# Hybrid decoder trunk on Trainium2: the first adaLN vectors summed by TensorE in place of VectorE and GpSimd

## The chip, the core and the metric

The kernel runs on one core of one Trainium2 chip. The metric is the device time of one execution in microseconds (us); less is better. Engines are named as in the profile: PE is TensorE (its matmuls), PEld TensorE's weight loads, DVE VectorE, ACT ScalarE, POOL GpSimd, and SP the engine whose queue issues most of the DMAs.

## What is computed

Two decoder layers on `x` (256 tokens by 1024 channels, f32). What matters here is how the first layer begins. The vector `c` (1024) goes through SiLU, and a 1024 x 6144 matrix makes six vectors of 1024 of it. The first two, shift and scale, are applied to the RMS-normalised `x`; the result `h` is the input of the first projection.

```
c_act = jax.nn.silu(c)
for layer in range(DEPTH):
    ada = c_act @ w_ada[layer] + b_ada[layer]
    sh1, sc1, g1, sh2, sc2, g2 = jnp.split(ada[:, None, :], N_ADA, axis=-1)
    h = rms_norm(x, norm_mix[layer]) * (1.0 + sc1) + sh1
    x = x + g1 * hybrid_mixer(h, w_in[layer], ...)
    h = rms_norm(x, norm_ffn[layer]) * (1.0 + sc2) + sh2
    x = x + g2 * f
```

`hybrid_mixer` projects `h` with `w_in` (1024 x 9232), runs forgetting attention and an HGRN2 recurrence on parts of the result, and projects back. `f` is a dense SwiGLU in layer 0 and a top-2-of-8 expert SwiGLU in layer 1.

## The kernel before, in words

Weights come from HBM as f32. Each is split into two parts of type fp32r: `halves` (L93) has ACT round the raw tile to `whi`, and `lower` (L97) has DVE subtract that from the raw tile to give `wlo`. A product is then three matmuls, high by high, high by low and low by high (`mm3`, L113 to L115, 512 columns wide, or `turned`, L411 to L413, 256 columns wide). The activations are split in the same way into `hTh` and `hTl`.

The first stage, `start` (L507 to L637), runs before the two things that every product needs are there: `h` needs shift and scale, and these need 8 MB of `w_ada`. So `start` works in four chunks of two blocks of 128 channels (`CHUNKS = (2, 2, 2, 2)`). For chunk q it loads two pieces of `w_ada` (1 MB each, scale then shift; channels of `c` on the partitions, eight rows k for each partition) and three pieces of `w_in` of 0.5 MB for three groups of output columns (`FIRST`). Loads go through SP's queue in program order, two chunks ahead; the raw tiles lie in a ring of eight, and a tile is loaded again when its last reader is done.

For each chunk the vectors are made in three steps before the change:

- `sums(q)`: DVE multiplies the eight rows of the scale piece by `silu(c)` and adds them up (L537, L539, 128 x 256 each), into `ac`.
- `shift_sums(q)`: POOL does the same for the shift piece, by one multiplication in place (L544, 128 x 2048) and three halving additions (L548).
- `columns(q)`: PE sums over the partitions, with the 128 x 128 blocks of `ac` as weights and a column of ones as the moving operand (L556): four f32 matmuls of one column, each of them two records in the trace.

`vectors(q)` then has DVE add the bias and multiply by the gain (L563, L565). ACT and DVE apply the vectors to the transposed, normalised `x` (L612, L614), ACT rounds (L615), DVE makes the low part (L617), and the products of the chunk follow: `products(q, 0)` with 12 matmuls of 512 columns, `products(q, 1)` with 24 of 256 columns, `products(q, 2)` with 12 of 512 columns. `turn(q + 1)` (L577, four transposes of `x`) and `columns(q + 1)` stand between the last two, so that the vectors of the next chunk come while `products(q, 2)` runs. `rows` (L570), `load_params` (L219 to L221) and `build_masks` (L159 to L192, on POOL) are helpers of the stage. `start` is written under a manual schedule: each engine gets its instructions in the order in which the code stands, and each engine works in order.

After the four chunks the mixer goes on with the next projection (`proj`), whose raw tiles come from four of the same ring's places. The layers behind it, in the order of the program, are the mixer, the dense part, the second mixer and the experts.

Of the kernel before, what the change touches and what calls it, by code (L numbers as in the profile page):

```python
# [14 lines left out]
OP = mybir.AluOpType  # L15
AX = mybir.AxisListType

P = 128
D = 1024
KD = D // P  # L20
# [20 lines left out]
def hybrid_trunk_kernel(  # L41
# [7 lines left out]
    v, a, pe, g = nc.vector, nc.scalar, nc.tensor, nc.gpsimd  # L49
# [7 lines left out]
    def acc_bank(name="acc"):  # L57
        return ps.tile([P, 512], F32, tag="acc", bufs=4, name=name)

    def t_bank(name="tb"):  # L60
        return ps.tile([P, 512], F32, tag="tb", bufs=4, name=name)
# [17 lines left out]
    def load_raw(src, nk, n, step=None):  # L79
        raw = raw_tile()  # L80
        if nk * n == 2048:
            raw = raw.rearrange("p (k n) -> p k n", k=nk)
        else:
            raw = raw.rearrange("p (k n) -> p k n", k=max(4, nk))[:, :nk, :n]
        for k in range(0, nk, step or nk):
            nc.sync.dma_start(out=raw[:, k:k + (step or nk)], in_=src[:, k:k + (step or nk)])
        return raw

    def halves(raw, room=None):

        hi, lo = room or (wp.tile([P, 2, 512], F32R, tag=t, bufs=NSP, name=t) for t in ("whi", "wlo"))
        hi, lo = hi[:, :raw.shape[1], :raw.shape[2]], lo[:, :raw.shape[1], :raw.shape[2]]
        a.copy(hi, raw)  # L93
        return raw, hi, lo

    def lower(raw, hi, lo):
        v.tensor_sub(lo, raw, hi.bitcast(F32))  # L97

    def pairs_of(w):
        return [(w[1][:, j], w[2][:, j]) for j in range(w[1].shape[1])]  # L100
# [47 lines left out]
    ones = const.tile([P, P], F32, name="ones")  # L148
# [48 lines left out]
    cact = const.tile([P, KD], F32, name="cact")  # L197
# [98 lines left out]
    def tmp(pool, name):  # L296
        return pool.tile([P, 512], F32, tag="tmp", bufs=4, name=name)
# [207 lines left out]
    def start(pool, hT, win):  # L505

        ring[0] = [wraw, (pool, "kq", 2), (pool, "ee", 2)]  # L507
        wa = w_ada[0].rearrange("(p k) n -> p k n", k=KD)
        wi = win.rearrange("(k p) n -> p k n", p=P)
        first = {c0: [acc_bank() for _ in range(NT)] for c0 in FIRST[:2]}  # L510
        first[FIRST[2]] = [t_bank() for _ in range(NT)]
        NQ = len(CHUNKS)
        first_of = [sum(CHUNKS[:q]) for q in range(NQ)]
        ld, acs, tps, mvs = {}, {}, {}, {}

        def load(q):
            kk, nb = first_of[q], CHUNKS[q]
            raws = []
            for comp in (1, 0):
                raws.append(load_raw(wa[:, :, D * comp + P * kk:D * comp + P * (kk + nb)], KD, P * nb))  # L520
                if q == 0 and comp == 1:
                    nc.sync.dma_start(out=xt, in_=x[0].rearrange("(i p) d -> p i d", p=P))
            ab = raw_tile()
            third = pool.tile([P, 1024], F32, tag=("lfh", "lfl")[q % 2], bufs=2, name="third")
            for c0, t in zip(FIRST, (ab[:, :1024], ab[:, 1024:], third)):
                t = t.rearrange("p (k n) -> p k n", k=2)[:, :nb]
                nc.sync.dma_start(out=t, in_=wi[:, kk:kk + nb, c0:c0 + 512])
                raws.append(t)
            ld[q] = raws

        def sums(q):

            raw, ac = ld[q][0], tmp(pool, "ac")[:, :P * CHUNKS[q]]
            acs[q] = [ac]
            for k in range(KD):
                if k == 0:
                    v.tensor_scalar(out=ac, in0=raw[:, 0], scalar1=cact[:, 0:1], scalar2=None, op0=OP.mult)  # L537
                else:
                    v.scalar_tensor_tensor(out=ac, in0=raw[:, k], scalar=cact[:, k:k + 1], in1=ac, op0=OP.mult, op1=OP.add)  # L539

        def shift_sums(q):

            w = ld[q][1]
            g.tensor_tensor(out=w, in0=w, in1=cact[:, :, None].to_broadcast([P, KD, P * CHUNKS[q]]), op=OP.mult)  # L544
            n = KD
            while n > 1:
                n //= 2
                g.tensor_add(w[:, :n], w[:, :n], w[:, n:2 * n])  # L548
            acs[q].append(w[:, 0])

        def columns(q):
            nb = CHUNKS[q]
            tp = mvs[q] = t_bank()
            for n in range(2):
                for b in range(nb):
                    pe.matmul(out=tp[:, nb * n + b:nb * n + b + 1], lhsT=acs[q][n][:, b * P:(b + 1) * P], rhs=ones[:, 0:1], start=True, stop=True)  # L556

        def vectors(q):
            kk, nb = first_of[q], CHUNKS[q]
            tp = mvs[q]  # L560
            for n, comp in enumerate((1, 0)):
                dst = ada[:, 0, comp, kk:kk + nb]
                v.tensor_add(dst, tp[:, nb * n:nb * (n + 1)], bcol[:, KD * comp + kk:KD * comp + kk + nb])  # L563
                if comp == 1:
                    v.scalar_tensor_tensor(out=dst, in0=dst, scalar=1.0, in1=gain_mix[0][:, kk:kk + nb], op0=OP.add, op1=OP.mult)  # L565

        def rows(k0, k1):
            for i in range(NT):
                cs = slice(P * k0, P * k1)
                a.activation(out=hT.xn[i][:, cs], in_=xt[:, i, cs], func=AF.Copy, scale=hT.r[i])  # L570

        def turn(q):
            tp = tps[q] = t_bank()
            for b in range(CHUNKS[q]):
                for i in range(NT):
                    kk = first_of[q] + b
                    pe.transpose(out=tp[:, (2 * b + i) * P:(2 * b + i + 1) * P], in_=hT.xn[i][:, kk * P:(kk + 1) * P], identity=ident)  # L577

        def products(q, n, w):
            bk = first[FIRST[n]]  # L580
            for c in range(4 if FIRST[n] == O_HQ else NT):
                for b in range(CHUNKS[q]):
                    k = first_of[q] + b
                    if FIRST[n] == O_HQ:
                        turned(bk, c, k, w[b], hT)
                    else:
                        mm3(bk[c], *hT.get(k, c), *w[b], k == 0, k == KD - 1)

        load(0)
        load(1)  # L590
        sums(0)
        for i in range(NT):
            for h in range(2):
                hT.square(i, h)
        for i in range(NT):
            hT.scale(i)
        rows(0, CHUNKS[0])
        shift_sums(0)
        load_params()
        turn(0)  # L600
        columns(0)
        rows(CHUNKS[0], KD)
        for q, nb in enumerate(CHUNKS):
            kk = first_of[q]
            w = [halves(ld[q][2])]
            if q:
                lower(*w[0])
            vectors(q)
            w.append(halves(ld[q][3]))
            hf = tmp(pool, "hf").rearrange("p (b t) -> p b t", b=2)[:, :nb]  # L610
            A, B = (ada[:, 0, j, kk:kk + nb] for j in (1, 0))
            a.activation(out=hf[:, 0], in_=tps[q][:, 0:S], func=AF.Identity, scale=A[:, 0:1], bias=B[:, 0:1])  # L612
            if nb > 1:
                v.tensor_scalar(out=hf[:, 1], in0=tps[q][:, S:2 * S], scalar1=A[:, 1:2], scalar2=B[:, 1:2], op0=OP.mult, op1=OP.add)  # L614
            a.copy(hT.hh[:, kk:kk + nb], hf)  # L615
            lower(*w[q > 0])
            v.tensor_sub(hT.hl[:, kk:kk + nb], hf, hT.hh[:, kk:kk + nb].bitcast(F32))  # L617
            if not q:
                lower(*w[1])
            products(q, 0, pairs_of(w[0]))  # L620
            w.append(halves(ld[q][4]))
            lower(*w[2])
            if q + 2 < NQ:
                load(q + 2)
            if q + 1 < NQ:
                sums(q + 1)
                shift_sums(q + 1)
            products(q, 1, pairs_of(w[1]))
            if q + 1 < NQ:
                turn(q + 1)  # L630
                columns(q + 1)
            products(q, 2, pairs_of(w[2]))
            if q == 0:
                load_late()
            if q == NQ - 2:
                build_masks(pool)
        ring[0] = [wraw]  # L637
        return first

# [1119 lines left out]
    ws = mixer(1, hT, {O_HI: banks[0]}, {O_HI + 512: banks[1]})  # L1759
# [8 lines left out]
CHUNKS = (2, 2, 2, 2)  # L1768
# [37 lines left out]
```

## Time and profile before

| what | value |
|---|---|
| device time, median of 3 runs | 1914.8 us (1912.79 to 1915.34) |
| the profiled execution's own time | 1916.2 us |
| its span in the trace | 1914.5 us |
| PE busy | 1845.4 us (96%) |
| DVE busy | 1569.5 us (82%) |
| ACT busy | 1309.9 us (68%) |
| POOL busy | 210.2 us (11%) |
| mean granted PE clock | 0.993 |
| read from HBM | 522.72 MB, 274 GB/s over the span |

The span runs from the first to the last instruction in the trace; 1.7 us of the profiled execution's own time lie around it. Busy time is a union over an engine's instructions. PEclk, the granted clock, is 1.00 at 2.4 GHz and 0.50 at 1.2 GHz; it is known from the first recorded change on, which in this trace is at 38.1 us, and shown as 1.00 ahead of that.

### The profile page before, as it was taken

Reading aid. Unit: us, or ns where it says so; the run is one execution under the profiler, and the core shown is the slowest. Engines: PE = TensorE matmul, PEld = TensorE weight load, DVE = VectorE, ACT = ScalarE, POOL = GpSimd, SP = SyncE. Lnnn points to the kernel's source line nnn. Section 1 sums busy time; section 2 is a strip of 40 time slices with the busy share of each in tenths; the row PEclk is TensorE's granted clock in tenths of the full one; section 3 lists DMA queues with packets and bytes.
Section 4 is the critical chain, followed back from the end, with each engine's and each line's share of the span. In section 5 each row is a group of like instructions: output and inputs, shape, how many; then the busy total and the mean of one; then the engine's idle time right before and its main releaser. Section 6 shows DMA issues by size and latency. Waiting matters only on the chain.

```text
span 1914.5 us, 25527 instructions
## 1 busy us (share of the span) xinstructions
PE 1845.4 (96%) x9510; PEld 1534.2 (80%) x9510; DVE 1569.5 (82%) x2006; ACT 1309.9 (68%) x1666; POOL 210.2 (11%) x184
## 2 busy tenths in 40 slices
PE   2999999999999999999999999999999999999998
PEld 2787788889978877788787888888888888888887
DVE  6878865878858887457898989999899989999997
ACT  2467568554436765595788787787887878878775
POOL 6701200000000012100001210003100021000000
PEclk9899999999999999999999999999999999999999
DMA  9543654888855425339899999999999999999990
GB/s 301 167 156 132 220 176 142 299 302 293 314 211 172 140 88 176 120 114 338 293 347 354 349 339 370 362 376 344 340 374 359 375 346 344 368 362 369 358 364 24
DMA packets 235140, 525.50 MB, mean 274 GB/s; under 512 B 11756, under 2 KB 23292, under 8 KB 235008
## 3 DMA queue, kind: packets, MB, share of 16 engines
q1 hardware_dynamic: 233624, 523.61, 76.3%
q8 instruction: 76, 1.25, 0.3%
q14 instruction: 56, 0.46, 0.1%
q10 hardware_dynamic: 1384, 0.18, 0.1%
HBM read 522.72 MB, written 1.05 MB: 274 GB/s over the span
## 4 chain that ended last, share of the span: by engine, by line
PE 74%; DVE 2%; ACT 2%; issue 1%; POOL 1%; DVEq 0%; ACTq 0%; POOLq 0%
PE acc L114 15%; PE acc L115 15%; PE acc L113 15%; PE yb L114 5%; PE yb L115 5%; PE yb L113 5%; PE acc L412 2%; PE acc L413 2%; PE acc L411 2%; PE tb L308 2%; DVE wlo L97 1%; PE tb L1560 1%; PE tb L798 1%; POOL rs L302 1%; PE tb L1290 1%
## 5 line engine op out<-in xcount | busy, mean ns | idle before, releaser
L97 DVE TENSOR_TENSOR wlo<-raw,whi 128x1024 fp32r<-128x1024 f32 (+1 forms) x888 | 1077.1, 1237 | 141.7 <-ACT whi L93 124.5
L93 ACT CAST whi<-raw 128x1024 fp32r<-128x1024 f32 (+1 forms) x888 | 919.3, 1047 | 315.3 <-PE acc L115 183.9
L113 PE MATMUL acc<-whi,g 128*128 128x512 f32 x880 | 349.2, 397 | 0.0
L115 PE MATMUL acc<-whi,g 128*128 128x512 f32 x880 | 344.2, 391 | 0.0
L114 PE MATMUL acc<-wlo,g 128*128 128x512 f32 x880 | 344.1, 391 | 0.0
L113 PE MATMUL acc<-whi,hTh 128*128 128x512 f32 x512 | 210.2, 414 | 4.1 <-ACT hTh L615 4.1
L114 PE MATMUL acc<-wlo,hTh 128*128 128x512 f32 x512 | 206.9, 405 | 5.2 <-DVE wlo L97 5.0
L115 PE MATMUL acc<-whi,hTl 128*128 128x512 f32 x512 | 206.6, 405 | 3.5 <-DVE hTl L617 3.5
L114 PEld LDWEIGHTS acc<-wlo,g 128*128 128x128 f32 x880 | 165.5, 188 | 35.9 <-DVE wlo L97 2.8
L115 PEld LDWEIGHTS acc<-whi,g 128*128 128x128 f32 x880 | 165.1, 188 | 35.7
L113 PEld LDWEIGHTS acc<-whi,g 128*128 128x128 f32 x880 | 165.4, 188 | 32.7
L114 PE MATMUL yb<-wlo,th 128*128 128x512 f32 x440 | 172.5, 392 | 4.1 <-DVE wlo L97 4.1
L115 PE MATMUL yb<-whi,tlo 128*128 128x512 f32 x440 | 171.6, 390 | 0.0
L113 PE MATMUL yb<-whi,th 128*128 128x512 f32 x440 | 171.6, 390 | 0.0
L114 PEld LDWEIGHTS acc<-wlo,hTh 128*128 128x128 f32 x512 | 98.2, 192 | 25.4 <-DVE wlo L97 7.5
L115 PEld LDWEIGHTS acc<-whi,hTl 128*128 128x128 f32 x512 | 97.6, 191 | 24.4 <-DVE hTl L617 5.3
L411 PE MATMUL acc<-hTh,whi 128*128 128x256 f32 x416 | 117.1, 282 | 0.0
L302 POOL TENSOR_TENSOR rs<-rs,mhalf 128x8 f32<-128x8 f32 (+1 forms) x28 | 48.1, 1719 | 623.9 <-DVE rs L301 614.9
L413 PE MATMUL acc<-hTh,wlo 128*128 128x256 f32 x416 | 116.5, 281 | 0.0
L412 PE MATMUL acc<-hTl,whi 128*128 128x256 f32 x416 | 116.3, 280 | 0.0
L113 PEld LDWEIGHTS acc<-whi,hTh 128*128 128x128 f32 x512 | 97.4, 191 | 22.4 <-ACT hTh L615 5.0
L114 PEld LDWEIGHTS yb<-wlo,th 128*128 128x128 f32 x440 | 82.6, 188 | 26.0 <-DVE wlo L97 9.3
(381 smaller groups left out, 2634.8 us busy)
## 6 DMA issues: line engine op xcount, KB each, us to landing
raw<-in_moe_w_gate SPq DMA_DIRECT2D x112, 1024.0 KB, 6.3
raw<-in_moe_w_up SPq DMA_DIRECT2D x112, 1024.0 KB, 5.9
raw<-in_moe_w_down SPq DMA_DIRECT2D x110, 1024.0 KB, 5.6
raw<-in_w_in SPq DMA_DIRECT2D x66, 1024.0 KB, 5.2
raw<-in_w_ada SPq DMA_DIRECT2D x48, 1024.0 KB, 6.8
raw<-in_dense_w_gate SPq DMA_DIRECT2D x10, 1024.0 KB, 8.1
raw<-in_dense_w_up SPq DMA_DIRECT2D x10, 1024.0 KB, 7.8
raw<-in_dense_w_down SPq DMA_DIRECT2D x10, 1024.0 KB, 8.8
```

What stands on the lines that cost most here:

```text
L93: a.copy(hi, raw)
L97: v.tensor_sub(lo, raw, hi.bitcast(F32))
L113: pe.matmul(out=o, lhsT=lh, rhs=rh, start=start, stop=False)
L114: pe.matmul(out=o, lhsT=lh, rhs=rl, start=False, stop=False)
L115: pe.matmul(out=o, lhsT=ll, rhs=rh, start=False, stop=stop)
L302: g.tensor_tensor(out=r, in0=r, in1=mhalf[:, :shape[1]], op=OP.pow)
L308: pe.transpose(out=tp[:, b * P:(b + 1) * P], in_=src(b), identity=ident)
L411: pe.matmul(out=o, lhsT=hi, rhs=hT.hh[:, k], start=(k == 0 and c % 2 == 0), stop=False)
L412: pe.matmul(out=o, lhsT=hi, rhs=hT.hl[:, k], start=False, stop=False)
L413: pe.matmul(out=o, lhsT=lo, rhs=hT.hh[:, k], start=False, stop=(k == KD - 1 and c % 2 == 1))
L798: pe.matmul(out=tv[:P - m, li, h, :].rearrange("p (b r) -> p b r", r=m), lhsT=el[:, :P - m], rhs=el.rearrange("p (b s r) -> p b s r", s=2, ...
L1290: pe.matmul(out=tp[:, b * 2 * P:(b * 2 + ne) * P], lhsT=src[:, i, kk * P:(kk + 1) * P], rhs=pair[0]["oneh"][:, i].rearrange("p n t -> p (n ...
```

## The change

The two partial sums on DVE and POOL (`sums`, `shift_sums`) go. `columns(q)` now sums over all 1024 channels by itself: for each of the four blocks of 128 output channels it issues eight f32 matmuls that accumulate in PSUM, with the raw `w_ada` block of row k as weights and column k of `silu(c)` as the moving operand. That makes 32 one-column matmuls for a chunk where there were 4.

The order is laid anew around it. A function `parts` makes both parts of one `w_in` piece. For chunk 0 the first piece is split ahead of the vectors, and the second behind `hTl`; from chunk 1 on the first two pieces are split right behind `columns` of that chunk, while `products` of the chunk before still run. The masks that POOL builds are written once, ahead of the chunks, where they stood behind chunk 2.

```diff
--- before.py
+++ after.py
@@ -511,7 +511,7 @@
         first[FIRST[2]] = [t_bank() for _ in range(NT)]
         NQ = len(CHUNKS)
         first_of = [sum(CHUNKS[:q]) for q in range(NQ)]
-        ld, acs, tps, mvs = {}, {}, {}, {}
+        ld, tps, mvs, ws = {}, {}, {}, {}
 
         def load(q):
             kk, nb = first_of[q], CHUNKS[q]
@@ -528,32 +528,14 @@
                 raws.append(t)
             ld[q] = raws
 
-        def sums(q):
-
-            raw, ac = ld[q][0], tmp(pool, "ac")[:, :P * CHUNKS[q]]
-            acs[q] = [ac]
-            for k in range(KD):
-                if k == 0:
-                    v.tensor_scalar(out=ac, in0=raw[:, 0], scalar1=cact[:, 0:1], scalar2=None, op0=OP.mult)
-                else:
-                    v.scalar_tensor_tensor(out=ac, in0=raw[:, k], scalar=cact[:, k:k + 1], in1=ac, op0=OP.mult, op1=OP.add)
-
-        def shift_sums(q):
-
-            w = ld[q][1]
-            g.tensor_tensor(out=w, in0=w, in1=cact[:, :, None].to_broadcast([P, KD, P * CHUNKS[q]]), op=OP.mult)
-            n = KD
-            while n > 1:
-                n //= 2
-                g.tensor_add(w[:, :n], w[:, :n], w[:, n:2 * n])
-            acs[q].append(w[:, 0])
-
         def columns(q):
+
             nb = CHUNKS[q]
             tp = mvs[q] = t_bank()
             for n in range(2):
                 for b in range(nb):
-                    pe.matmul(out=tp[:, nb * n + b:nb * n + b + 1], lhsT=acs[q][n][:, b * P:(b + 1) * P], rhs=ones[:, 0:1], start=True, stop=True)
+                    for k in range(KD):
+                        pe.matmul(out=tp[:, nb * n + b:nb * n + b + 1], lhsT=ld[q][n][:, k, b * P:(b + 1) * P], rhs=cact[:, k:k + 1], start=(k == 0), stop=(k == KD - 1))
 
         def vectors(q):
             kk, nb = first_of[q], CHUNKS[q]
@@ -586,54 +568,51 @@
                     else:
                         mm3(bk[c], *hT.get(k, c), *w[b], k == 0, k == KD - 1)
 
+        def parts(q, n):
+            w = halves(ld[q][2 + n])
+            lower(*w)
+            ws[q, n] = pairs_of(w)
+
         load(0)
         load(1)
-        sums(0)
         for i in range(NT):
             for h in range(2):
                 hT.square(i, h)
         for i in range(NT):
             hT.scale(i)
         rows(0, CHUNKS[0])
-        shift_sums(0)
         load_params()
         turn(0)
         columns(0)
         rows(CHUNKS[0], KD)
+        build_masks(pool)
         for q, nb in enumerate(CHUNKS):
             kk = first_of[q]
-            w = [halves(ld[q][2])]
-            if q:
-                lower(*w[0])
+            if not q:
+                parts(0, 0)
             vectors(q)
-            w.append(halves(ld[q][3]))
             hf = tmp(pool, "hf").rearrange("p (b t) -> p b t", b=2)[:, :nb]
             A, B = (ada[:, 0, j, kk:kk + nb] for j in (1, 0))
             a.activation(out=hf[:, 0], in_=tps[q][:, 0:S], func=AF.Identity, scale=A[:, 0:1], bias=B[:, 0:1])
             if nb > 1:
                 v.tensor_scalar(out=hf[:, 1], in0=tps[q][:, S:2 * S], scalar1=A[:, 1:2], scalar2=B[:, 1:2], op0=OP.mult, op1=OP.add)
             a.copy(hT.hh[:, kk:kk + nb], hf)
-            lower(*w[q > 0])
             v.tensor_sub(hT.hl[:, kk:kk + nb], hf, hT.hh[:, kk:kk + nb].bitcast(F32))
             if not q:
-                lower(*w[1])
-            products(q, 0, pairs_of(w[0]))
-            w.append(halves(ld[q][4]))
-            lower(*w[2])
+                parts(0, 1)
+            products(q, 0, ws.pop((q, 0)))
+            parts(q, 2)
             if q + 2 < NQ:
                 load(q + 2)
-            if q + 1 < NQ:
-                sums(q + 1)
-                shift_sums(q + 1)
-            products(q, 1, pairs_of(w[1]))
+            products(q, 1, ws.pop((q, 1)))
             if q + 1 < NQ:
                 turn(q + 1)
                 columns(q + 1)
-            products(q, 2, pairs_of(w[2]))
+                parts(q + 1, 0)
+                parts(q + 1, 1)
+            products(q, 2, ws.pop((q, 2)))
             if q == 0:
                 load_late()
-            if q == NQ - 2:
-                build_masks(pool)
         ring[0] = [wraw]
         return first
 
```

On PE, at the border of chunks 1 and 2 (the same three rows stand at each border and, ahead of the first product, in chunk 0): `tb<-ident,xn` are the transposes of `x`, the rows with one column are `columns`, and the rows behind them are `products(1, 2)`.

```order
 L412 MATMUL acc<-hTl,whi 128x256
 L413 MATMUL acc<-hTh,wlo 128x256
-L577 MATMUL tb<-ident,xn 128x128 x4
-L556 MATMUL tb<-ones,ac 128x1 x2
-L556 MATMUL tb<-ones,raw 128x1 x2
+L559 MATMUL tb<-ident,xn 128x128 x4
+L538 MATMUL tb<-cact,raw 128x1 x32
 L113 MATMUL tb<-whi,hTh 128x512
 L114 MATMUL tb<-wlo,hTh 128x512
```

The place is the same; 4 matmuls became 32, and the operand beside the weights is `cact`, that is `silu(c)`.

On DVE, in chunk 0, behind the parameters: `ada` rows are the vectors, `hf` is `h` in f32, `hTl` its low part, and `wlo` the low part of a `w_in` piece.

```order
-L563 TENSOR_TENSOR ada<-tb,bcol 128x2
-L565 SCALAR_TENSOR_TENSOR ada<-ada,prm 128x2
-L563 TENSOR_TENSOR ada<-tb,bcol 128x2
-L614 TENSOR_SCALAR hf<-tb,ada 128x256
-L97 TENSOR_TENSOR wlo<-raw,whi 128x1024
-L617 TENSOR_TENSOR hTl<-hf,hTh 128x512
+L97 TENSOR_TENSOR wlo<-raw,whi 128x1024
+L545 TENSOR_TENSOR ada<-tb,bcol 128x2
+L547 SCALAR_TENSOR_TENSOR ada<-ada,prm 128x2
+L545 TENSOR_TENSOR ada<-tb,bcol 128x2
+L598 TENSOR_SCALAR hf<-tb,ada 128x256
+L600 TENSOR_TENSOR hTl<-hf,hTh 128x512
```

The first `wlo` of the stage has moved from between `hf` and `hTl` to ahead of the vectors.

## Rows read from the trace of the kernel before

**Rows 1.** The page, part 2: busy tenths of PE in 40 slices.

```profile
PE   2999999999999999999999999999999999999998
```

**Rows 2.** Windows: stretch and length, then busy us (instructions) of each engine, PEclk, DMA, GB/s.

```profile
0.00:100.00 100.00, 60.93 (x292) 50.04 (x293) 72.10 (x84) 35.83 (x50) 67.69 (x86) 0.93 0.72 239
```

**Rows 3.** Timeline of PE, start to first product: start us, busy us, what [idle before <-releaser].

```profile
15.70 0.67 PE L219 MATMUL tb<-ident,mm 52*128 52x52 f32 x2 [15.70 <-DMA mm<-in_hg_lb]
...
17.24 0.85 PE L556 MATMUL tb<-ones,ac 128*128 128x1 f32 x4
24.15 1.01 PE L556 MATMUL tb<-ones,raw 128*128 128x1 f32 x4 [6.06 <-POOL raw L548]
27.56 0.79 PE L113 MATMUL acc<-whi,hTh 128*128 128x512 f32 x1 [2.40 <-ACT hTh L615]
```

**Rows 4.** Timeline of PE, end of chunk 0's second products to its third.

```profile
41.17 0.60 PE L577 MATMUL tb<-ident,xn 128*128 128x128 f32 x4
48.48 1.01 PE L556 MATMUL tb<-ones,ac 128*128 128x1 f32 x4 [6.71 <-DVE ac L539]
...
50.21 0.77 PE L113 MATMUL tb<-whi,hTh 128*128 128x512 f32 x1
50.78 0.63 PE L114 MATMUL tb<-wlo,hTh 128*128 128x512 f32 x1
51.21 0.63 PE L115 MATMUL tb<-whi,hTl 128*128 128x512 f32 x1
```

**Rows 5.** Timeline of PE, borders of chunks 1 to 3, and the end of the stage.

```profile
65.40 0.28 PE L413 MATMUL acc<-hTh,wlo 128*128 128x256 f32 x1
65.52 0.60 PE L577 MATMUL tb<-ident,xn 128*128 128x128 f32 x4
65.96 0.50 PE L556 MATMUL tb<-ones,ac 128*128 128x1 f32 x4
...
66.77 0.48 PE L113 MATMUL tb<-whi,hTh 128*128 128x512 f32 x1
...
75.75 0.60 PE L577 MATMUL tb<-ident,xn 128*128 128x128 f32 x4
...
88.60 0.39 PE L115 MATMUL tb<-whi,hTl 128*128 128x512 f32 x1
88.83 0.39 PE L113 MATMUL acc<-whi,hTh 128*128 128x512 f32 x1
```

**Rows 6.** Timeline of DVE: low parts of h and w_in, chunks 0 and 3.

```profile
26.77 4.52 DVE L97 TENSOR_TENSOR wlo<-raw,whi 128x1024 fp32r<-128x1024 f32 x1
...
79.02 1.21 DVE L97 TENSOR_TENSOR wlo<-raw,whi 128x1024 fp32r<-128x1024 f32 x1
80.15 0.72 DVE L617 TENSOR_TENSOR hTl<-hf,hTh 128x512 fp32r<-128x512 f32 x1
```

**Rows 7.** Timeline of SP: the loads for the projection behind the stage.

```profile
80.31 5.98 SPq L86 DMA_DIRECT2D raw<-in_w_in  x2
```

**Rows 8.** Windows around changes of the granted clock, in the first stage.

```profile
41.80:45.00 3.20, 0.00 (x0) 0.00 (x0) 3.13 (x3) 0.00 (x0) 3.04 (x3) 0.99 1.09 359
...
48.40:50.20 1.80, 1.72 (x8) 1.72 (x9) 1.80 (x2) 0.00 (x0) 1.80 (x1) 0.50 0.47 43
50.20:55.20 5.00, 5.00 (x13) 3.79 (x13) 4.97 (x4) 0.00 (x0) 4.91 (x2) 0.50 0.86 299
55.20:58.60 3.40, 1.04 (x4) 0.30 (x2) 2.71 (x5) 2.62 (x4) 3.25 (x3) 1.00 0.00 0
58.60:62.00 3.40, 3.16 (x8) 2.48 (x9) 3.26 (x7) 0.46 (x1) 3.33 (x7) 0.50 0.02 5
62.00:88.80 26.80, 26.15 (x160) 22.66 (x159) 20.45 (x32) 12.87 (x17) 24.08 (x49) 1.00 0.52 176
```

**Rows 9.** Timeline of PE: the longest one-sided run of narrow f32 matmuls (the router's).

```profile
905.05 1.85 PE L1036 MATMUL tl<-wr,xT 128*128 128x8 f32 x16
906.75 0.48 PE L113 MATMUL acc<-whi,yT 128*128 128x512 f32 x1
```

## The prediction, made before the changed kernel had run

> **What bounds the kernel now.** I read the page's slices first, then the first hundred microseconds closer and closer. PE is busy nine tenths or more in every slice but the first and the last [rows 1]. A window over the first 100 us has PE busy for 60.9 of them [rows 2]. So outside the start PE is the bound, and what the change is worth is the shift of one moment: the first product of the projection behind the stage, at 88.83 us [rows 5]. What stands behind it keeps its order but for some interleaving in the first mixer, so I take the shift as handed on whole.
>
> Where PE loses its 39 us is read in its timeline. It starts at 15.70, when the parameters land, does the transposes and the scale's columns by 18.1, and waits 6.06 us for POOL's shift sums until 24.15; its first product starts at 27.56 [rows 3]. Chunk 0's first two groups of products end at 41.17; then come the transposes, and PE waits 6.71 us for DVE's sums, with the third group beginning at 50.21 [rows 4]. From 62.0 on the stage is full: 26.15 us busy of 26.80 [rows 8]. So the waits that the change takes away lie in chunks 0 and 1; in chunks 2 and 3 PE has no hole to put anything into.
>
> **The cost of one columns matmul.** Eight records (four matmuls) take from 65.96 to 66.77, where the next product starts: 0.81 us [rows 5], and 48.48 to 50.21, 1.73 us, at granted clock 0.50 [rows 4, 8]. I read 0.107 us a record at 2.4 GHz and twice that at 1.2 GHz (the records start at that distance), that is 0.213 and 0.427 us a matmul. A product of 512 columns goes on every 0.23 us at 2.4 GHz, 88.60 to 88.83 [rows 5], and 0.43 us at 1.2 GHz, 50.78 to 51.21 [rows 4]; one of 256 every 0.12, 65.40 to 65.52 [rows 5]. So a matmul of one column is nearly as dear as one of 512, and 32 of them cost 6.83 us at the high clock and 13.66 at the low one, where 0.81 or 1.73 stood. By the figure of the Trainium skill for a stream of matmuls of up to 64 columns, about 25 ns each ("TensorE: Matmul & The Clock Gate", Back-to-back issue gap), the 64 records would take 1.6 us, and the sum would fall by over 5 us a chunk; the rows, with a weight load for each, say otherwise, and I go by them.
>
> **The clock.** Three chunks reach their columns straight from dense products, at 2.4 GHz. What a long run of one-column matmuls does to the clock no row of this trace shows: the longest narrow run is 1.70 us, 905.05 to 906.75, between dense products [rows 9]. The nearest rows: the clock fell 3.2 us after PE went idle at 41.8, and fell again at 58.6, with PE busy 1.04 of the 3.4 us ahead. It stayed low through 1.8 us of columns and then 5.0 us of products to 55.2, and rose the second time after products that filled 3.16 of 3.40 us [rows 8]. PE was busy nearly all of 48.4 to 51.8, columns and then products, about as full as 58.6 to 62.0, and yet no rise came at 51.8. I take from this that columns count for less than wide products, and choose that a run of them lets the clock fall as idling did, 3.2 us in. The bounds are never (the first rival) and at once.
>
> **The change part by part, likeliest case.**
> Gone: 8 small DVE sums and 4 large POOL operations a chunk. On PE's path they were the 6.06 and 6.71 us of waiting [rows 3, 4]; in chunks 2 and 3 they lay beside products, and their going is worth nothing there. POOL's load also stretched a low part on DVE to 4.52 us, where 1.21 is usual [rows 6]. That goes too. What is late next is the columns themselves.
> Chunk 0: PE is cold. The 32 matmuls start at 17.24, as now, and end at 17.24 + 13.66 = 30.9 (the shift piece is there by then: POOL's sums, done at 24.15 [rows 3], read it). From the last column to the first product it took 2.4 us (25.16 to 27.56, the last of the four records of 24.15 [rows 3]), so the first product starts at 33.3, against 27.56. `hTl` is ready some 3.9 us behind the columns, as in chunk 3, whose columns end at 75.75 + 0.44 + 0.81 = 77.0 [rows 5] and its `hTl` at 80.87 [rows 6]: 34.8, a wait of 0.65 us ahead of the third product. Wide products raise the clock after 5.0 or 3.4 us [rows 8]; I take 4.2. Until 37.5 some 8.3 of the 12 are done, the rest take 0.85: 38.35. The 24 of 256 columns: 41.15. Transposes 0.44 (65.52 to 65.96 [rows 5]): 41.6. Before, they began at 41.17: six microseconds of later start are given back by the shorter DVE chain.
> Chunk 1's columns: 3.2 us for 15 at the high clock, then 17 x 0.427 = 7.26: end at 52.05, against 50.21. `products(0, 2)` starts low: 9.8 products in 4.2 us, 2.2 x 0.23 = 0.5, so 4.7: 56.75. Chunk 1's 12 x 0.23 = 2.76 and 24 x 0.116 = 2.8, transposes 0.44: 62.75. A period is 10.46 + 4.7 + 2.76 + 2.8 + 0.44 = 21.16 us. Before, it was 10.23 in full chunks (65.52 to 75.75, transposes to transposes [rows 5]).
> Chunk 2's columns end at 73.2, chunk 3's at 94.36. Behind these come 4.7 + 2.76 + 2.8 + 2.76 = 13.0: the stage ends at 107.4, against 88.83, **18.6 us later**.
> The masks on POOL, moved ahead of the chunks: nothing, since POOL's sums are gone and the masks are first read past the stage; their selections ran beside DVE's low parts at the usual 1.21 us [rows 6]. If they stretched DVE, some tenths in `hTl`, beside a chunk of 21 us. The earlier splits: nothing, PE has no wait for `wlo` left in them. The loads: the SP queue keeps its order. A ring place now comes free when PE's columns are done instead of DVE's sums, one part of them behind chunk 3's columns; the last, that of chunk 3's `w_in`, comes with the low part behind them, some 9 us ahead of the end, as now (80.31 against 88.83 [rows 7, 5]). No gain, no loss; if a load came late, up to the 6 us of two issues.
>
> The profiled execution took 1916.2 us itself, 1.4 above the median of the runs; 1916.2 + 18.6 - 1.4 gives **1933.4 us**. The bounds inside this case: 3.4 or 5.0 us until the clock rises is -1.1 or +1.1 in three chunks; a fall at 2 or 5 us instead of 3.2 is up to 3 x 1.3 more or 3 x 1.8 less. So 1928 to 1937; a fall at once would add 3 x 3.2 us, at 1943, and I give that no more than the tail.
>
> **The rivals.**
> *The clock stays up in the columns, but they do not raise it.* For: it lived through the router's run, and PE is never idle in the columns. Against: the missing rise at 51.8. Chunk 0 is as above (41.6). Then a period is 6.83 for the columns, 2.76, a wait of 0.6 for `hTl` (now only partly hidden), 2.76, 2.8 and 0.44 = 16.2. Two of these and 6.83 + 2.76 + 0.6 + 2.76 + 2.8 + 2.76 = 18.5: the stage ends at 92.5, 3.7 later: **1918.5 us**.
> *The columns raise the clock and keep it up.* This is the case on the other side. From 15.70 PE then runs without a break, and at 4.2 us the clock rises, near 20. Chunk 0's columns end at 25.4: 6.5 matmuls at 0.427 and 25.5 at 0.213. First product 27.8, a wait of 1.0 for `hTl`, all at the high rate: transposes done at 34.9. Two periods of 16.2 and 18.5 end at 85.8, 3.0 earlier: **1911.8 us**. It decides by chunk 0's columns ending ahead of about 28 us: two of the three added microseconds in each later chunk must be won there. By the Trainium skill (same page, What's actually happening) the throttled clock is the default and sustained PE activity releases it; read plainly, the columns would do so, and this rival comes. The trace, with no rise at 51.8, speaks against the plain reading.
> *A mixture*, the clock falling in one or two chunks of three: each fall costs 3.6 us of columns and 1.9 of products, so 1924 or 1929.
>
> **How the numbers follow.** Fall in every chunk 0.62, stays up 0.17, mixture 0.10, raised 0.08, other 0.03. The range takes the first, the mixture, and most of the second: 1917 to 1937. A measurement tells some 0.2% from no change, here 3.8 us: below 1911.0 is faster, above 1918.6 slower. The raised case is mostly inside: faster 0.05. Same is the rest of it and half of the stays-up case, which lies on the border: 0.16. Slower 0.79.
>
> **What would show it.** Right: 256 records of L538, at 0.107 us apart and then 0.213 within one group; PEclk 0.50 ending each group of columns and in the first products behind it; chunk 1's columns beginning near 41.6 and ending near 52; no wait of PE for DVE or POOL above 2.5 us but the one ahead of the first product; the next projection at 107. Wrong: PEclk at 1.00 through all the columns (first rival), a rise ahead of the first product (second), columns at a quarter of the price, or time that is gained or lost behind the stage.

## The result and the profile after

| | before | changed |
|---|---|---|
| median of 4 runs each | 1913.8 us (1910.78 to 1915.34) | 1934.79 us (1933.03 to 1935.58) |
| the profiled execution's own time | 1916.2 us | 1933.03 us |
| its span | 1914.5 us | 1931.2 us |
| first product of the projection behind the stage | 88.83 us | 106.16 us |

The ratio of the runs is 1.011, with a 95% interval of 1.0093 to 1.0128: the change makes the kernel slower, by about 1%. Between the two profiled executions it is 1933.03 - 1916.2 = 16.8 us, and the stage's end has moved by 17.3 us. Nearly the whole shift was handed on. The medians lie further apart, 21.0 us: the profiled execution of before was 2.4 us above its median, that of the changed kernel 1.8 us below its own. Two of the twelve executions of the last version below (shared2_narrow) ran far longer at a lower granted clock (2994.21 and 2067.67 us); its median counts them, its ratio does not.

The page's slices of the changed kernel, the same part as [rows 1], with the row of the granted clock:

```profile
PE   6999999999999999999999999999999999999998
...
PEclk9799999999999999999999999999999999999999
```

PE's first slice went from 2 to 6 tenths: it is busier, and later. Only the second slice shows a granted clock under nine tenths; the clock of chunk 0 is not in this row, since the first recorded change is at 36.2 us here. The timeline of PE in the changed kernel, from its first work to the transposes behind chunk 0's products (fields as in [rows 3]):

```profile
14.96 0.67 PE L219 MATMUL tb<-ident,mm 52*128 52x52 f32 x2 [14.96 <-DMA mm<-in_hg_lb]
15.41 1.15 PE L559 MATMUL tb<-ident,xn 128*128 128x128 f32 x4
16.36 13.65 PE L538 MATMUL tb<-cact,raw 128*128 128x1 f32 x64
32.42 0.79 PE L113 MATMUL acc<-whi,hTh 128*128 128x512 f32 x1 [2.40 <-ACT hTh L599]
33.01 0.63 PE L114 MATMUL acc<-wlo,hTh 128*128 128x512 f32 x1
33.43 0.63 PE L115 MATMUL acc<-whi,hTl 128*128 128x512 f32 x1
...
39.76 0.60 PE L559 MATMUL tb<-ident,xn 128*128 128x128 f32 x4
```

Both waits of [rows 3, 4], 6.06 us for POOL and 6.71 us for DVE, are gone. In their place stand 13.65 us of columns in chunk 0, 64 records 0.21 us apart, the distance that went with granted clock 0.50 before [rows 4, 8], and one wait of 2.40 us ahead of the first product, as long as before. Two more waits of before are gone, for the low parts that DVE made beside POOL's sums:

```profile
31.35 0.80 PE L114 MATMUL acc<-wlo,hTh 128*128 128x512 f32 x1 [3.00 <-DVE wlo L97]
34.10 0.80 PE L115 MATMUL acc<-whi,hTl 128*128 128x512 f32 x1 [1.95 <-DVE hTl L617]
```

So the first product comes 4.9 us later than before (32.42, not 27.56), and yet the transposes behind chunk 0's products come at 39.76, where they stood at 41.17: up to here the change has cost nothing. The loss is made in the three borders that follow. Windows of the changed kernel, cut where the columns begin, where the clock falls, where the products begin and where the clock rises (fields as in [rows 2]):

```profile
40.20:43.00 2.80, 2.80 (x28) 2.80 (x27) 0.00 (x0) 0.00 (x0) 0.00 (x0) 1.00 0.58 98
43.00:51.14 8.14, 8.14 (x40) 8.14 (x40) 0.00 (x0) 0.00 (x0) 0.00 (x0) 0.50 1.06 364
51.14:56.66 5.52, 5.52 (x14) 4.36 (x15) 2.85 (x6) 2.14 (x4) 0.00 (x0) 0.50 0.23 89
56.66:62.55 5.89, 5.89 (x41) 5.40 (x41) 2.45 (x2) 2.09 (x2) 0.00 (x0) 1.00 0.01 3
62.55:66.90 4.35, 4.35 (x42) 4.35 (x40) 0.00 (x0) 0.00 (x0) 0.00 (x0) 1.00 0.76 241
66.90:72.09 5.19, 5.19 (x27) 5.19 (x26) 0.00 (x0) 0.00 (x0) 0.00 (x0) 0.50 0.00 0
72.09:77.14 5.05, 5.05 (x13) 3.99 (x14) 2.85 (x6) 2.13 (x3) 0.00 (x0) 0.50 0.00 0
83.20:87.38 4.18, 4.18 (x41) 4.18 (x39) 0.00 (x0) 0.00 (x0) 0.00 (x0) 1.00 0.00 0
92.92:97.62 4.70, 4.70 (x12) 3.73 (x13) 2.85 (x6) 2.13 (x3) 0.00 (x0) 0.50 0.74 236
```

PE is busy for all of every one of these stretches, and DVE and POOL do nothing while the columns run. Still the granted clock falls to 0.50 some 2.80 us into chunk 1's columns, 4.35 us into chunk 2's and 4.18 us into chunk 3's, and comes back only after 5.52, 5.05 and 4.70 us of wide products. The groups of chunks 2 and 3 in PE's timeline, with the transposes ahead of each, and the first product behind the stage:

```profile
62.11 0.60 PE L559 MATMUL tb<-ident,xn 128*128 128x128 f32 x4
62.55 9.68 PE L538 MATMUL tb<-cact,raw 128*128 128x1 f32 x64
...
82.77 0.60 PE L559 MATMUL tb<-ident,xn 128*128 128x128 f32 x4
83.20 9.85 PE L538 MATMUL tb<-cact,raw 128*128 128x1 f32 x64
...
106.16 0.39 PE L113 MATMUL acc<-whi,hTh 128*128 128x512 f32 x1
```

From border to border it is 22.35 us (39.76 to 62.11) and 20.66 us (62.11 to 82.77), against 10.23 for full chunks before [rows 5].

### The profile page after: what moved, and what is told of

Read it like the earlier page. It is cut to its first block, busy times and chain, and to the rows that moved or that the text cites. A ratio compares the mean times of both kernels' runs of the same rounds, so it can differ in the third digit from the quotient of the medians.

```text
span 1931.2 us, 25920 instructions
## 1 busy us (share of the span) xinstructions
PE 1884.4 (98%) x9734; PEld 1576.5 (82%) x9734; DVE 1533.5 (79%) x1974; ACT 1310.3 (68%) x1666; POOL 168.4 (9%) x168
## 4 chain that ended last, share of the span: by engine, by line
PE 74%; DVE 2%; ACT 2%; POOL 1%; issue 0%; DVEq 0%; ACTq 0%; POOLq 0%
PE acc L114 15%; PE acc L115 15%; PE acc L113 15%; PE yb L114 5%; PE yb L115 5%; PE yb L113 5%; PE acc L412 2%; PE acc L411 2%; PE acc L413 2%; PE tb L308 2%; DVE wlo L97 1%; PE tb L777 1%; PE tb L1539 1%; PE tb L1269 1%; POOL rs L302 1%
## 5 line engine op out<-in xcount | busy, mean ns | idle before, releaser
L113 PEld LDWEIGHTS acc<-whi,hTh 128*128 128x128 f32 x512 | 97.1, 190 | 20.2 <-ACT hTh L599 2.5
L115 PEld LDWEIGHTS acc<-whi,hTl 128*128 128x128 f32 x512 | 96.9, 189 | 19.4 <-issue 0.2
```

The lines of the kernel that those rows point to most:

```text
L113: pe.matmul(out=o, lhsT=lh, rhs=rh, start=start, stop=False)
L115: pe.matmul(out=o, lhsT=ll, rhs=rh, start=False, stop=stop)
```

## The experiments

The theory: the loss is the one-column matmuls themselves, 64 records a chunk, and the clock that they let fall; the order of the splits and masks is worth next to nothing. The rivals: the new order costs; or a weight load's price is all there is, whatever the clock.

**The new order without the new sums** (parts_alone). DVE's and POOL's sums and the masks' place are those of before.

```diff
-            w = [halves(ld[q][2])]
-            if q:
-                lower(*w[0])
+            if not q:
+                parts(0, 0)
...
                 turn(q + 1)
                 columns(q + 1)
-            products(q, 2, pairs_of(w[2]))
+                parts(q + 1, 0)
+                parts(q + 1, 1)
+            products(q, 2, ws.pop((q, 2)))
```

> DVE's and POOL's sums as before, the masks where they stood, and only the new order of the splits of w_in. Theory (the shift comes from the one-column matmuls and the clock behind them, the order is worth next to nothing): the next projection starts within 2 us of 88.8 us, time within 3 us of the kernel before. Rival (the new order is what costs, by splits that stand ahead of the vectors on ACT and DVE): most of the 17 us shift of the stage's end is here too, 1925 us or more.

Measured: 1914.77 us against 1914.72, ratio 0.9996 (0.9987 to 1.0005). PE's timeline, the first product behind the stage:

```profile
88.09 0.39 PE L113 MATMUL acc<-whi,hTh 128*128 128x512 f32 x1
```

That is 0.7 us ahead of 88.83. The rival of the order falls.

**The new sums without the new order** (sums_alone). The reverse: `columns` as changed; the splits and the masks stand as before.

```diff
-                    pe.matmul(out=tp[:, nb * n + b:nb * n + b + 1], lhsT=acs[q][n][:, b * P:(b + 1) * P], rhs=ones[:, 0:1], start=True, stop=True)
+                    for k in range(KD):
+                        pe.matmul(out=tp[:, nb * n + b:nb * n + b + 1], lhsT=ld[q][n][:, k, b * P:(b + 1) * P], rhs=cact[:, k:k + 1], start=(k == 0), stop=(k == KD - 1))
...
-        sums(0)
...
-        shift_sums(0)
...
```

> The sums on TensorE, and the old order of the splits and masks. Theory: the next projection starts 16 to 20 us later than before, near 106 us, as in the changed kernel, with PEclk 0.50 at the end of each group of columns; time within 3 us of the changed kernel's. Rival (the order costs): within 5 us of the kernel before.

Measured: 1933.34 us, ratio 1.0093 (1.0078 to 1.0108), which overlaps the changed kernel's interval. Its stage ends at

```profile
106.64 0.39 PE L113 MATMUL acc<-whi,hTh 128*128 128x512 f32 x1
```

Its clock falls in the same three borders (at 43.86, 67.76 and 88.24 us). The sums alone make the loss; the order and the masks add nothing that these runs can tell.

**The same weight loads with a wide moving operand** (wide). Each of the 32 matmuls streams `silu(c)`'s column 128 times over; one of the 128 equal results is read.

```diff
-                        pe.matmul(out=tp[:, nb * n + b:nb * n + b + 1], lhsT=ld[q][n][:, k, b * P:(b + 1) * P], rhs=cact[:, k:k + 1], start=(k == 0), stop=(k == KD - 1))
+                        pe.matmul(out=tp[:, P * (nb * n + b):P * (nb * n + b + 1)], lhsT=ld[q][n][:, k, b * P:(b + 1) * P], rhs=cact[:, k:k + 1].to_broadcast([P, P]), start=(k == 0), stop=(k == KD - 1))
...
```

> The changed kernel, but the moving operand of the 32 matmuls is silu(c)'s column repeated to 128 columns, of which one is read. Weight loads, their number and the record distance stay (f32 records of 128 columns go on every 0.11 us at 2.4 GHz in the trace of before). Theory (a run of matmuls of one column lets the clock fall because little streams through the array): granted clock 1.00 through the columns of chunks 1 to 3, each group 6.8 us instead of 9.7 to 11.1, the products behind them at 0.23 us; if chunk 0's columns raise the clock too, the stage ends near 86 us and the time is 3 us below before; if they don't, near 92 us and 3 us above. Rival (the clock falls from something else in these groups, the weight loads back to back, or the price of a weight load is all there is): PEclk and times as in the changed kernel or worse, 1934 us or more.

Measured: 1912.57 us, ratio 0.9988 (0.9979 to 0.9997), about 22 us less than the changed kernel, for an edit that adds 127 columns to each matmul. Windows over its four groups of columns, the first cut at 21.34 us, the first recorded change of the clock (ahead of it the field reads 1.00 in any case), then PE's timeline at the stage's end:

```profile
16.80:21.34 4.54, 4.54 (x23) 4.54 (x23) 1.23 (x1) 1.84 (x3) 4.13 (x13) 1.00 1.03 370
21.34:26.28 4.94, 4.94 (x44) 4.75 (x43) 0.00 (x0) 0.00 (x0) 4.46 (x15) 1.00 1.09 386
35.04:42.10 7.06, 7.06 (x66) 7.06 (x65) 0.06 (x1) 0.00 (x0) 4.37 (x14) 1.00 1.09 346
51.15:58.22 7.07, 7.07 (x67) 7.07 (x65) 0.00 (x0) 0.00 (x0) 0.00 (x0) 1.00 0.42 148
67.28:74.35 7.07, 7.07 (x66) 7.07 (x65) 0.00 (x0) 0.00 (x0) 0.00 (x0) 1.00 0.74 248
```

```profile
86.14 0.39 PE L113 MATMUL acc<-whi,hTh 128*128 128x512 f32 x1
```

The groups of chunks 1 to 3 take 7.06 us at granted clock 1.00 (64 records at 0.11 us), and in chunk 0 the clock rises 4.54 us into the columns, which take 9.48 us instead of 13.65. Number and place of the weight loads are the same, PE is as busy, and the clock stays up: of the two kernels, only the one in which a single column streams loses the clock. So the loss divides like this: with the clock up from the middle of chunk 0's columns on, the change is worth the 2.7 us by which this stage ends sooner than before (88.83 - 86.14); the low clock costs 106.16 - 86.14 = 20.0 us. The time is 2.2 us below before, where 3 were expected.

**Chunk 0's columns first** (wide_early). As wide; PE sums chunk 0 ahead of the parameters and the transposes.

```diff
+        columns(0)
         load_params()
         turn(0)
-        columns(0)
```

> As the one before, with chunk 0's columns ahead of the parameters and the transposes of x in PE's order, so that they start when the first piece of w_ada is there (9 to 10 us) instead of at 16.4. Theory: chunk 0's columns end near 19 to 20 us, the first product comes near 23 to 24 instead of 32.4, and the stage ends near 81 to 83 us; time 6 to 8 us below before. Rival (the second piece of w_ada lands too late, or the splits of w_in are not there): first product at 27 us or later, the same time as the one before.

Measured: 1909.56 us, ratio 0.9971 (0.9959 to 0.9983). The columns start at 9.96, when the first piece lands, and end at 20.12; the first product comes at 24.43 instead of 28.68 in wide:

```profile
9.96 10.22 PE L538 MATMUL tb<-cact,raw 128*128 128x128 f32 x64 [9.96 <-DMA raw<-in_w_ada]
20.12 0.50 PE L219 MATMUL tb<-ident,mm 52*128 52x52 f32 x2
20.45 0.60 PE L559 MATMUL tb<-ident,xn 128*128 128x128 f32 x4
24.43 0.79 PE L113 MATMUL acc<-whi,hTh 128*128 128x512 f32 x1 [3.38 <-ACT hTh L599]
25.03 0.63 PE L114 MATMUL acc<-wlo,hTh 128*128 128x512 f32 x1
25.45 0.63 PE L115 MATMUL acc<-whi,hTl 128*128 128x512 f32 x1
```

The stage ends at 83.90, a little later than I gave it: the vectors waited for the parameters, 3.38 us instead of 2.40, and the products behind that wait go on every 0.43 us, at the low clock. The time is 5.2 us below before, less than the 6 to 8 I had given.

**The work shared between TensorE and DVE** (shared). From chunk 1 on DVE sums the scale piece as before the change; PE sums only the shift piece, 16 matmuls of 128 columns, then two for DVE's partial sums. POOL sums nothing.

```diff
+            if q + 1 < NQ:
+                sums(q + 1)
             products(q, 1, ws.pop((q, 1)))
...
+                    if n == 0 and q in acs:
+                        pe.matmul(out=o, lhsT=acs[q][:, b * P:(b + 1) * P], rhs=ones, start=True, stop=True)
+                        continue
```

> As wide_early, but from chunk 1 on DVE sums the scale piece as before the change (eight operations, then two f32 matmuls), and TensorE only the shift piece, with 16 matmuls of 128 columns; POOL sums nothing. Theory: a group of columns costs 3.4 + 0.5 us instead of 7.1 on TensorE, and DVE, with no POOL beside it, takes 4 us for its sums, ahead of need: three groups give 3 x 3.2 = 9.6 us, the stage ends near 74 us, time near 1900 us. Rival (DVE's sums are late again, or chunk 2's and 3's loads are, now that TensorE comes for them sooner): a wait of 2 us or more ahead of the columns' last matmuls, the stage ends at 80 us or later, time 1906 us or more.

Measured: 1899.72 us, ratio 0.9921 (0.9907 to 0.9935). DVE's timeline, its sums for chunk 2, then PE's, the first product and the one behind the stage:

```profile
42.23 0.38 DVE L536 TENSOR_SCALAR ac<-raw,cact 128x256 f32<-128x256 f32 x1
42.65 3.61 DVE L538 SCALAR_TENSOR_TENSOR ac<-raw,cact,ac 128x256 f32<-128x256 f32 x7
```

```profile
24.91 0.79 PE L113 MATMUL acc<-whi,hTh 128*128 128x512 f32 x1 [3.38 <-ACT hTh L614]
...
74.47 0.39 PE L113 MATMUL acc<-whi,hTh 128*128 128x512 f32 x1
```

DVE's sums are in time: they take 4.0 to 4.3 us, the longest beside POOL's mask selections, where those of chunk 1 took 10.6 us before, beside POOL's sums (37.86 to 48.42). PE has no wait at the borders.

**The parameters between the two halves** (shared2). As shared, with this order in chunk 0:

```diff
-        columns(0, (0, 1))
+        columns(0, (0,))
         load_params()
+        columns(0, (1,))
         turn(0)
```

> As shared, with the parameters' transposes between the two halves of chunk 0's columns instead of behind them. Theory: the vectors no longer wait for the parameters, the first product comes some 1 us sooner than in shared (near 23.4 us), the clock does not fall ahead of it, and 1 to 3 us more are gained. Rival (the parameters' rows land only near 15 us and hold up the shift half, or the vectors wait for the transposes of x anyway): the same time as shared, or 1 us more.

Measured: 1897.56 us, ratio 0.9909 (0.9894 to 0.9924). PE's timeline, its two first groups, the first product and the end of the stage:

```profile
8.38 6.22 PE L553 MATMUL tb<-cact,raw 128*128 128x128 f32 x32 [8.38 <-DMA raw<-in_w_ada]
14.53 0.50 PE L219 MATMUL tb<-ident,mm 52*128 52x52 f32 x2
14.86 3.76 PE L553 MATMUL tb<-cact,raw 128*128 128x128 f32 x32
18.46 0.60 PE L574 MATMUL tb<-ident,xn 128*128 128x128 f32 x4
21.20 0.50 PE L113 MATMUL acc<-whi,hTh 128*128 128x512 f32 x1 [2.14 <-ACT hTh L615]
...
68.66 0.39 PE L113 MATMUL acc<-whi,hTh 128*128 128x512 f32 x1
```

The first product is at 21.20, sooner than the 23.4 I expected, since the first piece landed sooner too (columns from 8.4 us, not 10.4). The stage ends at 68.66, 20.2 us before the one of before; the profiled executions differ by 19.4 us, the medians by 17.4. Against shared, the wait ahead of the first product is shorter (2.14 us, not 3.38), and the clock stays up behind it: the products go on every 0.23 us (22.27 to 22.50), where shared's go on every 0.43 (25.50 to 25.93). But the first landings differ by a microsecond or two between executions, the profiled execution of shared was the slowest of its five, and the two intervals overlap, so how much of the 2.2 us between the medians the order brought is not shown. This version beats both kernels.

**The last version with one moving column** (shared2_narrow). Is it the sharing, or the width?

```diff
-                        pe.matmul(out=o, lhsT=ld[q][n][:, k, b * P:(b + 1) * P], rhs=cact[:, k:k + 1].to_broadcast([P, P]), start=(k == 0), stop=(k == KD - 1))
+                        pe.matmul(out=o, lhsT=ld[q][n][:, k, b * P:(b + 1) * P], rhs=cact[:, k:k + 1], start=(k == 0), stop=(k == KD - 1))
...
```

> As shared2, with one moving column in place of 128, so that runs of one-column matmuls are 3.9 us long in chunks 1 to 3 (at 2.4 GHz) instead of the changed kernel's 6.8. Theory: chunk 0's two groups no longer raise the clock and cost 13.7 us in all instead of 9.5, so the first product comes near 25.5 us instead of 21.2; in the later chunks the clock may fall once or not at all ahead of the products, since in the changed kernel it fell 2.8 to 4.4 us into a group; stage's end 73 us without a fall, 76 to 79 with a fall in each; time 1901 to 1908 us. Rival (the sharing alone is what gives shared2 its time, the width nothing): stage's end within 1 us of shared2's 68.7 us, time near 1898 us.

Measured: 1909.8 us, ratio 0.9977 (0.9968 to 0.9986). The stage ends at 81.83. The rival falls by 12 us. My own numbers were 2 to 3 us too small: the clock fell in all three borders (at 35.68, 52.75 and 69.81 us), and each fall cost more than the 1 to 2 us that I had allowed for it. PE's timeline at the second border, then windows cut where the clock falls and rises there:

```profile
49.29 3.66 PE L553 MATMUL tb<-cact,raw 128*128 128x1 f32 x32
52.81 0.99 PE L550 MATMUL tb<-ones,ac 128*128 128x1 f32 x4
53.66 0.77 PE L113 MATMUL tb<-whi,hTh 128*128 128x512 f32 x1
```

```profile
49.29:52.75 3.46, 3.46 (x34) 3.46 (x32) 0.43 (x1) 0.00 (x0) 0.00 (x0) 1.00 0.62 202
52.75:59.58 6.83, 6.83 (x20) 5.57 (x20) 4.01 (x9) 2.54 (x4) 0.00 (x0) 0.50 0.18 68
```

Chunk 2's group still runs fast (32 records in 3.52 us), but the clock falls with its end: the four records behind take 0.85 us, and the products go at the low rate. Width is worth 12 of shared2's 17 us.

## Why the prediction was right

The forecast was 1933.4 us, slower; measured were 1934.79 us and 1.011. The mechanism came as forecast: the columns at about their price, and a fall of the clock in all three borders. That the sum came so close is in part luck. By its steps:

- **The price of a one-column matmul.** 13.66 us were worked out for chunk 0, 13.65 came. The Trainium skill's figure of about 25 ns for such matmuls back to back ("TensorE: Matmul & The Clock Gate", Back-to-back issue gap), which the prediction set against the rows, would by estimate have made it 1.6 us. The trace disagrees: with a weight load for each, the shortest group of 64 records took 9.54 us in the changed kernel.
- **The fall of the clock** was put 3.2 us into each group, from an idle stretch. It came 2.80, 4.35 and 4.18 us in. With 10.46 worked out for each group, 10.94, 9.54 and 9.72 came, in sum 1.2 us less.
- **The rise** was put 4.2 us into the products; it took 5.52, 5.05 and 4.70 us in the borders, so that the 12 products took 5.27 us behind chunk 1's columns (51.14 to 56.41), and 5.17 and 5.00 us behind the next two, where 4.7 were given: in sum 1.3 us more, which cancels the 1.2 us of the columns. In chunk 0 the rise took 3.8.
- **Chunk 0** was too slow in the sum: chunk 1's columns at 41.6, where 40.20 came. 0.9 us is the earlier start of chunk 0's columns (16.36, not 17.24), most of it the parameters' landing (14.96, not 15.70). The other half microsecond lies in the first 12 products: a wait of 0.65 us for `hTl`, carried over from chunk 3, did not come (the third product follows the second after 0.42 us), and the clock rose somewhat sooner. The new order, which moved the split from between `hf` and `hTl`, is the smaller part of that: in sums_alone, where the split still stands there, the third product follows the second after 0.52 us (32.85 to 33.37).
- **The stage's end**: 107.4 worked out, 106.16 measured, a shift of 17.3 instead of 18.6 us; nearly all of the difference is chunk 0's. The time is nearer to the forecast than the shift is, since the medians lie 21.0 us apart, and the traces explain 17.3 of these; the rest is scatter between executions, and no trace here shows where it arose. That the masks and the splits cost nothing is borne out by the two runs that part order and sums; that the loads don't, by PE's timeline, which has no wait in the three borders.
- **The rivals** fell, but the sum of the second was right. It has the clock raised and kept up by the columns, and was worked out at a stage's end of 85.8 and 1911.8 us; wide, which makes this happen, has 86.14 and 1912.57. Read plainly, the rule of the Trainium skill beside it ("TensorE: Matmul & The Clock Gate", What's actually happening: activity releases the throttle) would have had the narrow columns do this. The trace disagrees: through 13.65 us without a gap, at 100% busy, chunk 0's records stayed 0.21 us apart. No run has the case of the first rival, in which the clock stays up but is not raised.

What decided between the rivals was the missing rise at 51.8 in the trace of before. The sums of DVE and POOL were late in two chunks, and the prediction priced the cure by what PE has to carry in all four.

## What to carry to other kernels

A sum over partitions on TensorE with many weights and one moving column costs a weight load for each, and it can cost the clock of what stands behind it; price both from rows, and count them where PE is the bound, not where it waits. If such a run can't be avoided, repeat the moving column: here 128 columns went in nearly the time of one (0.11 us a record) and took 22 us off. Better still is to give PE only the part that the other engines can't deliver in time.

## What the hardware showed that I had not expected

- The granted clock fell in stretches in which PE was 100% busy throughout (40.20 to 51.14 and 62.55 to 72.09 us). Busy time in the profile did not tell that the clock would hold.
- An f32 matmul of 128 moving columns took about 3% longer than one of one column, weight load included: 7.06 us for 64 records, against 6.83 at the distance of 0.107 us. Widening was nearly free here.
- Even behind a group of 32 one-column records the clock fell: in chunk 2 of the last run 3.46 us from its start, just ahead of its end, and in chunk 3 at 69.81, 0.70 us into the products behind it.
